# Output projection by seven block products, its sums prepared in the attention stage, two blocks of results added by DMAs

## The chip, the cores and the metric

One core of one Trainium2 chip runs the whole program. The metric is the device time of one execution in microseconds. The core has a matrix engine (PE, with its weight loads as PEld), a vector engine (DVE), a scalar engine (ACT), a general engine (POOL), and an engine that issues DMAs (SP). Each takes its own instructions in order and waits for the others by semaphores. PE writes to eight banks of PSUM, each 128 x 512 fp32.

## The reference

One decoder layer on 1024 positions with width 1024, all fp32:

```python
h = rms_norm(x, ln_pre_mix[l])
proj = h @ w_in[l]                       # pooling channels (256), then q, k, v of 12 heads of 64
...
pool_out = multi_scale_pool(u_pool, w_pool[l], pool_scale[l])
attn_out = dilated_attention(q, k, v).reshape(B, S, ATTN_WIDTH)
mix = jnp.concatenate([pool_out, attn_out], axis=-1) @ w_out[l]
x = x + rms_norm(mix, ln_post_mix[l])
h = rms_norm(x, ln_pre_ffn[l])
f = (jax.nn.silu(h @ w_gate[l]) * (h @ w_up[l])) @ w_down[l]
x = x + rms_norm(f, ln_post_ffn[l])
```

The change concerns the line with `w_out`: a 1024 x 1024 matrix times the 1024 mixed channels of 1024 positions.

## The kernel before

Everything lies channels by positions: a tile has 128 channels (a chunk) on its partitions and 512 positions (half h = 0 or 1) in its rows. Each fp32 factor is split into a high part (what the matrix engine's reduced fp32 keeps) and a low part (the rest), and a product is three matrix instructions: high by high, high by low, low by high (`PASSES`). ACT makes high parts, DVE or POOL low parts, by a subtraction (`split`, line 335; on POOL it is cut into two instructions of 512 columns).

The program runs in four stages.

1. **Projections and attention**, 0 to about 410 us. There are twelve units (pair of heads, half); each makes scores, exponents, turned exponents and products with v. A plan gives each unit's steps times in units (`put`, line 1184; the numbers are in the table `PRM`), and `emit` (line 1135) sorts all steps by these times. That sort is the order of each engine's instructions. Dense work that needs no fresh attention result (projections of the next pair, and at the end the output projection) is dealt between the steps as fill (`Fill`, line 595).
2. **Output projection** (`out_proj`, line 1271): for each half h and each 128 output channels d, eight input chunks k by three passes, so 24 instructions of 128 x 512 that collect in one bank, 192 for a half. Half 0 is fill in the last units, with its chunk 7 (from the last pair) last. Half 1 comes after the attention, from 414 to 460 us. Each result bank is copied by ACT to `z[h](d)` in SBUF (line 1298). The input chunks are written by `into` as high and low parts, sent to memory by `to_memory` (`mixd`) and fetched by `mixed` when their room comes free; only chunk 7 stays in SBUF.
3. **Norm and residual** (`chain`, line 1397): `Squares` sums the squares of a half's eight rows (ACT squares, DVE adds), PE's product with a column of ones gives the mean, ACT, POOL and PE turn it into a row of factors (`rsqrt_mean`, line 358: the power -1/2 is one POOL instruction), `add(d)` scales z and adds x on DVE (lines 1410, 1411), `parts(d)` makes the parts of the scaled sum for the next stage, and `whole(d)` its squares and scaled copy. For half 0 this runs beside the second half of the output projection; for half 1 it runs beside the first feature products. In half 1, ACT squares the projection's results straight from the banks.
4. **Features (SwiGLU)**: 2816 features in pairs j of blocks, by seven block products of quarter size in place of eight (`seven`, line 1588). For the first six pairs, the product that needs only half 0 of the positions is made first (`firsts`, line 1484; 48 instructions a pair, first with the four upper input chunks, block row kh = 0, then with the lower). The list that is handed to `emit` at line 1708 sets their order.

SP's order is set by the same sort, so a DMA that waits for its source holds back those behind it.

## Time and profile before

| what | us |
|---|---|
| median of three runs (lowest, highest) | 1110.75 (1110.72, 1111.95) |
| the profiled execution | 1109.44 |
| its span on the core (rest lies around it: 1.84) | 1107.6 |
| PE busy in the span | 1093.1 |
| DVE, ACT, POOL busy | 784.7, 550.3, 528.8 |
| stretch 100 to 400 us (attention): PE, DVE, ACT, POOL busy of 300 | 295.5, 242.4, 212.5, 128.0 |
| stretch 400 to 460 us (end of attention, second half of the projection): the same, of 60 | 60.0, 44.3, 39.9, 7.6 |
| stretch 460 to 530 us (first feature products): the same, of 70 | 70.0, 63.9, 43.4, 5.0 |

A row of the timeline reads: start and duration in us, engine, line, operation, output from input by the program's names, size, and the count of instructions in the row. Its duration runs to the modelled end of the last; the pace of a row of PE is found from the start of the next row. In a table of windows, "(x304)" is the number of instructions, and PEclk the granted clock of PE as a share of full speed.

### The profile page before, as it was taken

The page shows a single profiled execution, that of the slowest core. Times are in us where ns is not written, and L with a number is a line of the kernel's source. Part 1 is how long each engine was busy: PE and PEld are TensorE (multiplying, and loading weights), DVE is VectorE, ACT ScalarE, POOL GpSimd, SP SyncE. Part 2 cuts the span into 40 slices and gives each one's busy share as a digit, 9 for nine tenths or more (in the row PEclk, how much of TensorE's full clock was granted, in tenths as well). Part 3 has the DMA queues.
Part 4 walks back from the last instruction along what each step waited for, and adds up shares of the span by engine and source line. Part 5 has one row for each costly group of instructions (what it writes and reads, how often), then busy time and mean ns, then how long its engine had stood idle before and what let it go on. Part 6 is the DMA issues. An engine that isn't in the chain of part 4 may idle for free.

```text
span 1107.6 us, 16113 instructions
## 1 busy us (share of the span) xinstructions
PE 1093.1 (99%) x5694; PEld 932.1 (84%) x5694; DVE 784.7 (71%) x1356; ACT 550.3 (50%) x985; POOL 528.8 (48%) x425
## 2 busy tenths in 40 slices
PE   9999999999999999999999999999999999999997
PEld 7888899989888888888888888888888888888896
DVE  7967978787988767799777777677566462343684
ACT  7456767676777755866322222333222543343442
POOL 0111617263554021100567777576568986666521
PEclk9999999999999999999999999999999999999999
DMA  8325242425149437664466666543445895656442
GB/s 295 96 75 189 96 134 75 155 70 178 55 156 336 154 142 288 240 228 156 160 235 238 238 238 237 199 171 124 152 185 210 285 353 194 208 180 201 133 153 77
DMA packets 91297, 201.82 MB, mean 182 GB/s; under 512 B 9296, under 2 KB 25168, under 8 KB 89808
## 3 DMA queue, kind: packets, MB, share of 16 engines
q1 hardware_dynamic: 90240, 200.00, 51.4%
q8 instruction: 45, 0.74, 0.3%
q10 hardware_dynamic: 976, 0.79, 0.2%
q14 instruction: 36, 0.29, 0.1%
HBM read 143.87 MB, written 56.89 MB: 181 GB/s over the span
## 4 chain that ended last, share of the span: by engine, by line
PE 89%; DVE 5%; ACT 2%; POOL 2%; DMA 1%; issue 1%; ACTq 0%; DVEq 0%; POOLq 0%
PE ps_pj L292 26%; PE ps_s L292 25%; PE ps_o L292 25%; PE ps_t L292 10%; PE ps_t L295 2%; POOL whl L340 1%; DMA v<-vd 1%; DVE pp L912 1%; DVE ptr L966 0%; DVE ql L561 0%; ACT ptr L965 0%; DMA wraw<-in_w_in_dram 0%; DVE rsw L529 0%; DVE qh L560 0%; ACT pp L830 0%
## 5 line engine op out<-in xcount | busy, mean ns | idle before, releaser
L292 PE MATMUL ps_o<-tT,fw 128*128 128x512 f32 x648 | 150.4, 389 | 0.0
L292 PEld LDWEIGHTS ps_o<-tT,fw 128*128 128x128 f32 x648 | 121.6, 188 | 25.2
L292 PE MATMUL ps_pj<-x,whl 128*128 128x512 f32 x480 | 131.4, 399 | 0.2 <-DVE whl L340 0.2
L1482 POOL TENSOR_TENSOR fw<-rw,fw 128x512 fp32r<-128x512 f32 x72 | 99.0, 1397 | 30.4 <-ACT fw L1480 28.9
L292 PEld LDWEIGHTS ps_pj<-x,whl 128*128 128x128 f32 x480 | 86.4, 188 | 14.6 <-DVE whl L340 0.7
L340 POOL TENSOR_TENSOR whl<-wraw,whl 128x512 fp32r<-128x512 f32 x44 | 60.2, 1389 | 67.0 <-ACT whl L336 62.3
L1777 POOL TENSOR_TENSOR op<-rw,op 128x512 fp32r<-128x512 f32 x38 | 62.2, 1637 | 32.7 <-ACT op L1776 32.3
L366 POOL TENSOR_TENSOR nrr<-nrr,half 128x4 f32<-128x4 f32 (+1 forms) x7 | 6.9, 985 | 141.8 <-ACT eps L365 99.2
L292 PE MATMUL ps_s<-b,fw 128*128 128x512 f32 x312 | 72.5, 389 | 0.0
L1482 POOL TENSOR_TENSOR whl<-rw,whl 128x512 fp32r<-128x512 f32 x30 | 47.8, 1613 | 45.5 <-ACT whl L1480 30.8
L292 PEld LDWEIGHTS ps_s<-b,fw 128*128 128x128 f32 x312 | 58.6, 188 | 12.1
L1776 ACT ACTIVATE op<-rw 128x1024 fp32r<-128x1024 f32 x38 | 40.0, 1058 | 57.3 <-PE ps_t L292 29.8
L1480 ACT ACTIVATE fw<-rw 128x1024 fp32r<-128x1024 f32 x45 | 47.5, 1061 | 38.6 <-PE ps_o L292 15.5
L292 PE MATMUL ps_pj<-whl,x 128*128 128x256 f32 (+1 forms) x432 | 64.7, 298 | 0.0
L966 DVE TENSOR_TENSOR ptr<-ps_t,ptr 128x512 fp32r<-128x512 f32 (+1 forms) x84 | 52.9, 647 | 15.1 <-ACT ptr L965 14.7
L965 ACT ACTIVATE ptr<-ps_t 128x512 fp32r<-128x512 f32 (+1 forms) x84 | 45.2, 561 | 32.9 <-PE ps_t L295 23.5
L292 PEld LDWEIGHTS ps_pj<-whl,x 128*128 128x128 f32 x432 | 57.3, 191 | 2.2
L1778 DVE TENSOR_TENSOR op<-rw,op 128x512 fp32r<-128x512 f32 x33 | 28.9, 875 | 40.7 <-ACT op L1776 36.6
L1777 POOL TENSOR_TENSOR fw<-rw,fw 128x512 fp32r<-128x512 f32 x26 | 42.6, 1640 | 21.1 <-ACT fw L1776 20.5
L830 ACT ACTIVATE pp<-pp,sx 128x256 f32<-128x256 f32 x96 | 47.8, 501 | 8.2 <-DVE sx L827 7.7
L292 PE MATMUL ps_o<-ptr,v 128*128 128x128 f32 (+3 forms) x376 | 50.5, 268 | 1.2 <-DVE ptr L966 0.8
L292 PE MATMUL ps_pj<-b,fw 128*128 128x512 f32 x216 | 50.3, 389 | 0.0
(337 smaller groups left out, 2780.9 us busy)
## 6 DMA issues: line engine op xcount, KB each, us to landing
rw<-bd SPq DMA_DIRECT2D x77, 256.0 KB, 3.9
rw<-in_w_gate_dram SPq DMA_DIRECT2D x28, 512.0 KB, 4.7
rw<-in_w_up_dram SPq DMA_DIRECT2D x28, 512.0 KB, 6.0
v<-vd SPq DMA_DIRECT2D x22, 512.0 KB, 4.9
rw<-wsd SPq DMA_DIRECT2D x44, 256.0 KB, 3.8
bd<-p SPq DMA_DIRECT2D x39, 256.0 KB, 2.4
rw<-in_w_down_dram SPq DMA_DIRECT2D x33, 256.0 KB, 3.8
wraw<-in_w_out_dram SPq DMA_DIRECT2D x15, 512.0 KB, 5.3
```

Of the source, the lines that this page charges most:

```text
L292: return tc.keep_in_program_order(nc.tensor.matmul(*a, **k))
L295: return tc.keep_in_program_order(nc.tensor.transpose(dst, src, by))
L340: pin(eng.tensor_tensor(dst[:, 1, at:at + w], src[:, at:at + w], dst[:, 0, at:at + w].bitcast(F32), ALU.subtract))
L830: nc.scalar.activation(pt[:, j, lo:], pt[:, j, lo:], AF.Exp, bias=sx[:, 0, side, j, hd, 0:1], scale=-1.0, accum_out=sx[:, 0, side, j, hd, ...
L912: nc.vector.tensor_scalar(pv, pv, un.wv[:, side, j, hd:hd + 1], None, op0=ALU.mult)
L965: nc.scalar.activation(ptr[:, 0, :w], t[:, :w], AF.Copy)
L966: nc.vector.tensor_tensor(ptr[:, 1, :w], t[:, :w], ptr[:, 0, :w].bitcast(F32), ALU.subtract)
L1480: nc.scalar.activation(dst[:, :, 0], src, AF.Copy)
L1482: low[0] = eng.tensor_tensor(dst[:, i, 1], src[:, i], dst[:, i, 0].bitcast(F32), ALU.subtract)
L1776: nc.scalar.activation(w[:, :, 0], raw, AF.Copy)
L1777: nc.gpsimd.tensor_tensor(w[:, 0, 1], raw[:, 0], w[:, 0, 0].bitcast(F32), ALU.subtract)
L1778: (nc.gpsimd if p == "P1" else nc.vector).tensor_tensor(w[:, 1, 1], raw[:, 1], w[:, 1, 0].bitcast(F32), ALU.subtract)
```

## The change

The 1024 x 1024 product is written as 2 x 2 blocks of 512 (output channels, input channels, positions) and made by seven products of such blocks in place of eight. Four are of weight and input sums (S1 by T1, S2 by T2, S3 by T3, S4 by B22), three of blocks themselves (A11 by B11, A12 by B21, A22 by T4). Each is 4 output tiles i by 4 chunks c by 3 passes, so 48 instructions and 336 in all, where there were 384.

- **Order of products.** P5, P3, P1, P6, P7 (240 instructions, list `early`) are the fill of the last units; P2, P4 (96, `later_on`) come after the attention, where half 1 stood. Half 1 of the positions is block column 1, half 0 is block column 2. Half 0 is complete after the early products, half 1 only with P2 and P4.
- **Input sums.** `finish` runs when a chunk of 128 channels is done (pooling chunks 0 and 1, pairs 2 to 7). It makes that chunk's blocks and sums, their parts, and sends them to memory (`mixd`, now seven blocks by four chunks). Values of other chunks that a sum needs come back from memory by `other_chunks` (`vald`, `t2d`). The table 'se' says which engine, DVE (1) or POOL (0), makes each. Two tiles, `job` and `val`, exist once each.
- **Weight sums.** `weight_sums` reads w_out, makes the four sums S1 to S4 on POOL, four times four instructions of 128 x 512, in the same tile `job`, and sends them to memory (`wod`) during the attention. `out_weights` fetches weights for two output tiles at a time and splits them by 'oe' on DVE or POOL.
- **Results.** `out_done`: a product that comes first for a z row is copied there by ACT; later ones are added by DVE. P2 and P4 are copied by ACT to the tile `late`, and four DMAs on POOL's queue add it to half 1's z in SBUF (`accum_op`), two rows each. The squares of half 1 are taken from z after that, through one tile, `rb`.
- **Moved.** `whole`, the mean and its row of half 0 go from beside the projection to beside the first feature products. These are ordered in groups: for pairs 0 to 2 the products with kh = 0, then those with kh = 1, then pairs 3 to 5 as before. Table `PRM`: several hundred planned times and engine choices are new.

```diff
- 'c0': (0.14731, 0.21299, 0.22594, 0.57089, 0.30506, 0.69439, 0.95539, 0.04332),
- 'ft': ('pj', 't', 's', 'pj', 't', 's'),
+ 'c0': (0.24652, 0.35, 0.44694, 0.95, 0.1, 0.1745, 0.26633, 0.28),
+ 'ft': ('t', 's', 'pj', 't', 's', 'pj'),
...
+ 'se': {'B11': (1, 0, 0), 'B22': (1, 0, 0, 0, 0), 'B21': (1, 1, 0)},
...
+ 'oe': (0, 1, 0, 0, 1, 0, 0, 0, 0, 0, 1, 0, 0, 1),
+ 'zp': 200}
...
+    def finish(k, h, val):
+
+        c, v = k % 4, val.bitcast(F32)
+        if k < 4:
+            nc.sync.dma_start(vald[h, c], v)
+            did(("val", h, c))
+            if h == 0:
+                return
+        t = job["t"]
+        x = [t[:, i].bitcast(F32) for i in range(2)]
+        name = "B11" if k < 4 else "B21" if h else "B22"
+        eng = [nc.vector if i else nc.gpsimd for i in G["se"][name]]
+        hl = att.tile([P, 2, 512], F32R, name="mix", tag="mix", bufs=1)
+        halved(hl[:, 0], hl[:, 1], v, eng[0])
+        ship(name, c, hl.rearrange("p a t -> p (a t)"))
+        if name == "B22":
+            eng[1].tensor_tensor(x[0], v, x[0], ALU.subtract)
+            eng[2].tensor_tensor(x[1], x[0], x[1], ALU.add)
+            nc.sync.dma_start(t2d[c], x[1])
+            did(("t2", c))
+            halved(t[:, 2], t[:, 0], x[0], eng[3])
+            ship("T3", c, t[:, 2], t[:, 0])
+            halved(t[:, 3], val, x[1], eng[4])
+            ship("T2", c, t[:, 3], val)
+            return
+        i = k if k < 2 else 0
+        eng[1].tensor_tensor(x[i], *((x[i], v) if name == "B11" else (v, x[i])), ALU.subtract)
+        halved(t[:, 2 + i], t[:, i], x[i], eng[2])
+        ship("T1" if name == "B11" else "T4", c, t[:, 2 + i], t[:, i])
...
+    def weight_sums(i):
...
+            nc.gpsimd.tensor_tensor(to, a, b, op)
+        nc.sync.dma_start(wod[i].rearrange("p n m -> p (n m)"), r.rearrange("p f m -> p (f m)"))
...
+    early = [(p, i) for p, j in (("P5", 2), ("P5", 0), ("P3", 0), ("P3", 2)) for i in (j, j + 1)]
+    early += [(p, i) for j in (0, 2) for p in ("P1", "P6", "P7") for i in (j, j + 1)]
...
+    later_on = [(p, i) for p in ("P2", "P4") for i in range(4)]
...
+    def out_done(p, i, ps, done):
+
+        def plus(h, d):
+            with tc.high_priority(offset=G["zp"]):
+                nc.vector.tensor_tensor(z[h](d), ps, z[h](d), ALU.add)
...
+        if p in ("P2", "P4"):
+            d = i + 4 * (p == "P4")
+            if i == 0:
+                late["y"] = fw([P, 4, 512], F32, "late")
+            nc.scalar.activation(late["y"][:, i], ps, AF.Copy)
+            if i % 2:
+                with tc.high_priority(offset=G["zp"]):
+                    nc.gpsimd.dma_start(z[1](d - 1, 2), late["y"][:, i - 1:i + 1], accum_op=ALU.add)
+                for e in (d - 1, d):
+                    done(e, z[1](e))
...
+                if (p, i) == ("P1", 0):
+                    for x in range(2):
+                        fetch_block("T2", x, xroom(6, 7))
...
-    sqs = [(Squares(), Squares(tag=("o", "pj")[h], to=eps[:, 4 * h:4 * h + 4])) for h in range(2)]
+    sqs = [(Squares(jk=(("p", 2), ("rb", 1))[h]), Squares(tag=("o", "pj")[h], to=eps[:, 4 * h:4 * h + 4])) for h in range(2)]
...
-    st, weights = out_proj(1, 3, sqs[1][0].add)
-    weights(3)
-    *chain0, mean0, rows0 = chain(0, *sqs[0], G["c0"])
-    emit((st, 0.0, 1.0), *chain0, mean0)
+    for n in range(2):
+        fetch_block("T4", n, lambda n: big(4 + n, [P, 2, 2, 512], F32R, "t4"))
+    st = out_proj(later_on, sqs[1][0].add)
+    *chain0, whole0, mean0, rows0 = chain(0, *sqs[0], G["c0"])
+    emit((st, 0.0, 1.0), *chain0)
...
-    emit(([x for f in before for x in f], 0.0, 1.0), (two[0], 1.0, 1.0 + part), (two[1], 1.0 + part, 1.0 + 2 * part),
-         *chain(1, *sqs[1], G["c1"]), rows0,
+    emit(([x for n in (0, 8) for f in before[:3] for x in f[n:n + 8]] + [x for f in before[3:] for x in f], 0.0, 1.0), (two[0], 1.0, 1.0 + part), (two[1], 1.0 + part, 1.0 + 2 * part),
+         *chain(1, *sqs[1], G["c1"]), whole0, mean0, rows0,
```

In instructions of the whole program: PE has 48 fewer matrix instructions of 512 columns; DVE goes from 1334 to 1313, ACT from 848 to 855, POOL from 430 to 503 (four of them the DMAs), SP from 522 to 592.

**First place: the fetch of T2 near the end of the attention.** SP in the kernel after; `fw` four times are B11 and T3, `m_4574` and `m_4576` the two halves of T2, `m_4054` the end of B22:

```order
L986 DMA t2d<-job 128x512
L965 DMA mixd<-job 128x512 x3
L965 DMA mixd<-val 128x512
L1346 DMA m_4054<-mixd 128x1024
L1368 DMA wraw<-wod 128x2x512
L955 DMA job<-t2d 128x512
L1346 DMA fw<-mixd 128x2x1024 x4
L1368 DMA wraw<-in_w_out_dram 128x2x512
L1346 DMA m_4574<-mixd 128x2x1024
L1346 DMA m_4576<-mixd 128x2x1024
```

Before, SP fetched the mixed chunks of half 1 there, with no writes of sums between them:

```order
L332 DMA wraw<-in_w_out_dram 128x1024 x3
L1262 DMA fw<-mixd 128x2x1024 x3
L332 DMA wraw<-in_w_out_dram 128x1024 x2
L931 DMA mixd<-mix 128x1024
L1262 DMA fw<-mixd 128x1024
```

T2's two halves now stand behind five other transfers in that queue.

**Second place: the two means of the projection.** PE in the kernel after, from the end of the early products on. The first row is the last 24 instructions of P7 and the first 24 of P2; the rows with `fw,ow` are the rest of P2, `t_4960` and `t_4962` are the block T4 of P4. Behind the rows shown stand the other 36 of P4, then 72 feature instructions, and then the mean of half 1:

```order
L305 MATMUL ps_pj<-fw,whl 128x512 x48
L305 MATMUL ps_o<-ones,sq 128x1 x4
L305 MATMUL ps_pj<-fw,ow 128x512 x10
L308 MATMUL ps_o<-idt,nrr 128x128 x4
L305 MATMUL ps_pj<-fw,ow 128x512 x14
L305 MATMUL ps_pj<-t_4960,whl 128x512 x6
L305 MATMUL ps_pj<-t_4962,whl 128x512 x6
```

and ACT there, the last squares of half 1 (`rb`), with those of half 0 (`p<-z`), scaled copies (L1533) and feature weights (L1585) between them:

```order
L1482 ACTIVATE rb<-z_4601 128x512
L1482 ACTIVATE p<-z_4131 128x512
L1585 ACTIVATE fw<-rw 128x2x512
L1533 ACTIVATE z_4131<-z_4131,g3s 128x512 x2
L1482 ACTIVATE rb<-z_4601 128x512
L1585 ACTIVATE fw<-rw 128x2x512
L1482 ACTIVATE rb<-z_4601 128x512 x2
L1604 ACTIVATE q<-ps_s 128x512 x2
L377 ACTIVATE nrr<-ps_o 128x4
```

Before, the last two squares of half 1 came straight from the banks, one of them behind half 0's mean:

```order
L1376 ACTIVATE p<-ps_pj 128x512
L361 ACTIVATE nrr<-ps_o 128x4
L365 ACTIVATE eps<-ps_o 128x4
L1298 ACTIVATE z_4851<-ps_s 128x512
L1376 ACTIVATE p<-ps_s 128x512
```

The work on half 0's rows, of which most stood beside the projection, now stands ahead of half 1's last squares on ACT.

**Third place: POOL from the last weights of the projection to the powers.** After:

```order
L356 TENSOR_TENSOR ow<-wraw,ow 128x512 x2
L356 TENSOR_TENSOR whl<-wraw,whl 128x512 x2
L1402 DMA z_4600<-late 128x1024
L382 TENSOR_TENSOR nrr<-nrr,half 128x4
L1402 DMA z_4600<-late 128x1024
L1402 DMA z_4601<-late 128x1024
L1587 TENSOR_TENSOR whl<-rw,whl 128x512 x2
L1587 TENSOR_TENSOR fw<-rw,fw 128x512 x2
L1402 DMA z_4601<-late 128x1024
L382 TENSOR_TENSOR nrr<-nrr,half 128x4 x2
```

Before, the three powers stood together there, behind the last splits of projection weights:

```order
L340 TENSOR_TENSOR whl<-wraw,whl 128x512 x2
L914 TENSOR_SCALAR pp<-pp,wv 128x256 x15
L340 TENSOR_TENSOR whl<-wraw,whl 128x512 x4
L366 TENSOR_TENSOR nrr<-nrr,half 128x4 x3
L1482 TENSOR_TENSOR fw<-rw,fw 128x512 x2
```

The first power now stands behind a DMA that adds to z, the next two behind four of them.

316 lines of the change are left out of this document (175 added, 141 removed), and 272 rows, old and new, of the table PRM.

## The prediction

> **What bounds the kernel now.** First the page's busy times and chain:
>
> ```profile
> PE 1093.1 (99%) x5694; PEld 932.1 (84%) x5694; DVE 784.7 (71%) x1356; ACT 550.3 (50%) x985; POOL 528.8 (48%) x425
> PE 89%; DVE 5%; ACT 2%; POOL 2%; DMA 1%; issue 1%; ACTq 0%; DVEq 0%; POOLq 0%
> ```
>
> PE bounds the whole, so a PE instruction taken away is worth its pace wherever PE then finds its factors. The windows say where that is:
>
> ```profile
> 100.00:400.00 300.00, 295.47 (x1908) 264.73 (x1908) 242.40 (x632) 212.46 (x509) 128.01 (x141) 1.00 0.40 140
> 385.00:390.00 5.00, 5.00 (x28) 4.13 (x27) 4.86 (x14) 2.53 (x7) 2.01 (x5) 1.00 1.03 421
> 400.00:460.00 60.00, 60.00 (x304) 50.72 (x303) 44.34 (x61) 39.90 (x65) 7.55 (x5) 1.00 0.63 233
> 460.00:530.00 70.00, 70.00 (x318) 57.93 (x318) 63.87 (x100) 43.44 (x71) 4.96 (x4) 1.00 0.54 194
> ```
>
> Columns are busy us (and count) of PE, PEld, DVE, ACT, POOL, then granted clock, DMA share, GB/s. From 400 to 530 PE never waits and POOL is nearly idle; DVE has 91% from 460 on. The clock is full, so no term of clock enters.
>
> The pace of a dense instruction of 512 columns, from the starts of two rows of the timeline:
>
> ```profile
> 483.98 11.04 PE L292 MATMUL ps_s<-b,fw 128*128 128x512 f32 x48
> 494.86 1.52 PE L292 MATMUL ps_pj<-b,fw 128*128 128x512 f32 x6
> ```
>
> (494.86 - 483.98) / 48 = 0.2267 us.
>
> **The change part by part.**
>
> *Fewer products.* 384 become 336. 48 x 0.2267 = **-10.9**. All stand in dense fill or in the dense stretch behind the attention.
>
> *The fetch of T2.* SP issues it behind B11 and T3 (4 MB) and 0.5 MB of weights. Those wait for room that the last scores leave. In before the same room is released so, and the end of the attention has these rows:
>
> ```profile
> 378.74 0.28 PE L292 MATMUL ps_s<-k,ql 128*128 128x256 f32 x1
> ...
> 390.96 1.03 PE L295 MATMUL ps_t<-idt,pp 128*128 128x128 f32 x8
> 391.75 3.01 PE L292 MATMUL ps_s<-m,whl 128*128 128x512 f32 x12
> 394.60 0.87 PE L292 MATMUL ps_o<-ptr,v 128*128 128x128 f32 x8
> 395.30 0.85 PE L292 MATMUL ps_o<-ptr,vlast 128*128 128x128 f32 x8
> ...
> 379.98 1.40 SPq L1262 DMA_DIRECT2D fw<-mixd  x3
> ...
> DMA to landing us min/median/max: 4.8/6.9/8.8
> ```
>
> The first megabyte lands 4.8 us after its issue, and at 421 GB/s each further one takes 2.5 (1.049 MB / 421); the extremes 4.8 and 8.8 of the three, issued 0.9 apart, bear that out. So T2's first half, with 4.5 MB ahead of it, lands 4.8 + 3 x 2.5 + 1.2 + 2.5 = 16.0 after the issue, and the issue follows the last scores (end 379.0) by about 1.0: **17.0**. PE wants it behind 48 instructions of 512 columns (10.9), 26 of attention products (0.70 per eight, the starts of 394.60 and 395.30: 2.3) and 16 turns (0.79 per eight: 1.6), with 0.2 for two small ones: **15.0**. That is +2.0; bounds 0 (PE is late itself) and 4 (the writes of sums take bandwidth too).
>
> *The end of the early products to the first rows.* Call the end of P7 E. In before the chain of half 0's norm is, from mean to first sum:
>
> ```profile
> 421.00 0.95 PE L292 MATMUL ps_o<-ones,sq 128*128 128x1 f32 x8
> 424.68 0.60 PE L295 MATMUL ps_o<-idt,nrr 128*128 128x128 f32 x4
> 425.31 5.36 DVE L1410 SCALAR_TENSOR_TENSOR z<-z,g2s,ps_o 128x512 f32<-128x512 f32 x8 [3.84 <-PE ps_o L295]
> 430.59 4.89 DVE L1411 TENSOR_TENSOR z<-z,xr 128x512 f32<-128x512 f32 x8
> 435.40 1.21 DVE L340 TENSOR_TENSOR whl<-wraw,whl 128x1024 fp32r<-128x1024 f32 x1
> 436.54 0.74 DVE L1421 SCALAR_TENSOR_TENSOR b<-z,g3s,b 128x512 fp32r<-128x512 f32 x1
> 440.21 4.05 DVE L1421 SCALAR_TENSOR_TENSOR b<-z,g3s,b 128x512 fp32r<-128x512 f32 x6
> ```
>
> PE does 24 of P2 first (mean at E+5.4), then 10 more beside the mean's way through ACT and POOL (0.8 + 2.3: row at E+8.5), and DVE starts 0.6 behind, at E+9.2. It does eight scalings at 0.66 (5.28 to the next start), eight sums at 0.60 (4.81) and the split of the weights for P4's tiles 2 and 3 (1.14): done at E+20.4. PE wants that low part behind 72 instructions and the small ones, at E+17.9: a stall of **2.5**; in before, such splits stood one in front of the other with banks to spare.
>
> *The mean of half 1.* In before it came without a wait:
>
> ```profile
> 457.56 0.95 PE L292 MATMUL ps_o<-ones,sq 128*128 128x1 f32 x8
> ```
>
> After, PE reaches it behind 96 instructions of P2 and P4, 72 of features and the small ones: 168 x 0.2267 = 38.1, plus 1.1, so E+39.2 without stalls. It needs eight squares of half 1, and ACT makes the last of them behind all that stands ahead in its order. ACT's prices, as intervals between starts:
>
> ```profile
> 436.10 0.63 ACT L1376 ACTIVATE p<-z 128x512 f32<-128x512 f32 x1
> 436.62 0.60 ACT L1376 ACTIVATE p<-ps_s 128x512 f32<-128x512 f32 x1
> 437.10 0.61 ACT L1298 ACTIVATE z<-ps_pj 128x512 f32<-128x512 f32 x1
> 437.57 3.80 ACT L1420 ACTIVATE b<-z,g3s 128x512 fp32r<-128x512 f32 x6
> 441.25 0.60 ACT L1298 ACTIVATE z<-ps_s 128x512 f32<-128x512 f32 x1
> ```
>
> A square is 0.52, a copy from a bank 0.48, a scaled part (3.68 / 6) 0.61; scaled copies to z are taken as the same. A split of weights is 0.95:
>
> ```profile
> 456.54 1.05 ACT L1480 ACTIVATE whl<-rw 128x1024 fp32r<-128x1024 f32 x1
> 457.49 0.58 ACT L1376 ACTIVATE p<-ps_s 128x512 f32<-128x512 f32 x1
> ```
>
> The first part can start with the first finished sum, at E+9.2 + 5.3 + 0.6 = E+15.1. From there to the last square ACT has 8 parts (4.9), 16 squares of both halves (8.3), 8 scaled copies (4.9), 8 weight splits (7.6), three copies to `late` and two results (2.4): 28.1 us, so E+43.2, and the last addition and its release bring E+44.1. That is **4.9** behind E+39.2, with the 2.5 above inside it. If ACT and DVE hand the one `rb` tile to and fro with a wait each time (an addition of 0.6 behind each of the later squares, about half seen by ACT), it is 2 more, 6.9; if ACT finds its work in less than these sums, nothing: bounds 0 and 7.8. DVE alone has 31.8 us by the same rows from E+9.2 (E+41), so ACT ends last. I take the sum that needs no hand-over, 4.9.
>
> *Additions by DMA.* Four on POOL's queue, 512 KB each. No row shows such a DMA. Nearest: a power on POOL, and writes of that size and less.
>
> ```profile
> 422.24 1.02 POOL L366 TENSOR_TENSOR nrr<-nrr,half 128x4 f32<-128x4 f32 x1 [2.45 <-ACT nrr L361]
> ...
> mixd<-mix SPq DMA_DIRECT2D x14, 512.0 KB, 4.4
> bd<-p SPq DMA_DIRECT2D x39, 256.0 KB, 2.4
> ```
>
> Landing within 4.4 us, the first lies ready at E+16 or so and the last before ACT comes to its squares (E+41), so 0. If POOL is held by an issue ahead of a power, up to 2 (a power is 1.0 us long here); below zero no reason. I take 0, as the power waits for PE's mean behind 24 products anyway. The Trainium skill, "DMA: Bandwidth & Descriptors", section on the anatomy of a DMA from GpSimd, gives 2.0 us plus bytes by 436 GB/s; by it an estimate is 3.2 us each, and the sum would be the same.
>
> *The attention.* DVE loses 20 low parts of `mix` and some splits and gains sums, about 10 us less. ACT has 6 more. POOL gains 44 instructions of sums and parts, 8 weighings and 10 splits:
>
> ```profile
> L340 POOL TENSOR_TENSOR whl<-wraw,whl 128x512 fp32r<-128x512 f32 x38 | 51.1, 1366 | 34.4 <-ACT whl L336 29.8 <-issue 4.6
> L914 POOL TENSOR_SCALAR pp<-pp,wv 128x256 f32<-128x256 f32 x46 | 24.6, 553 | 50.1 <-DVE wv L883 50.1
> ```
>
> 54 x 1.37 + 8 x 0.55 = 78 us more on POOL, so 128 + 78 = 206 of 300. PE there runs under its dense pace already, and its idle of 4.5 us in the window is the least that lighter DVE could give back: between -3 and +6, from what hides it (POOL has 94 us left) to what shows (next part). Taken as 0.
>
> *At no cost:* new banks for the first features and groups of three pairs (the same 288 instructions), and `whole` of half 0 later (its 8 additions lie in DVE's 31.8).
>
> Sum: -10.9 + 2.0 + 4.9 = **-4.0**. The profiled 1109.44 becomes 1105.4; the median of the runs lies 1.3 above the profiled one, so **1106.7**.
>
> **The rivals.**
>
> *Nearly the whole saving arrives.* The means and T2 are hidden after all: ACT's squares come early since PE itself ran late. For it: PE at 60.00 and 70.00 of 60 and 70, so before had slack in every hand-over there. Against: DVE's 63.87 of 70. Time: 1110.75 - 10.9 = 1099.9, to 1102 with half of one stall.
>
> *The saving is eaten.* Hand-over by one `rb` tile (6.9), T2 at its 4: -10.9 + 10.9 = 0, 1110.8.
>
> *POOL gates the attention (slower).* In before, a DVE addition took twice as long while POOL split:
>
> ```profile
> 416.25 3.54 POOL L340 TENSOR_TENSOR whl<-wraw,whl 128x512 fp32r<-128x512 f32 x2 [3.51 <-ACT whl L336]
> 418.56 1.78 DVE L1377 TENSOR_TENSOR sq<-sq,p 128x512 f32<-128x512 f32 x1
> 439.00 1.28 DVE L1377 TENSOR_TENSOR sq<-sq,p 128x512 f32<-128x512 f32 x2
> ```
>
> 1.78 against 0.61 to 0.64. The added 62 instructions of two inputs or weighings, each making one DVE instruction about 0.7 to 1.1 longer, are 43 to 68 us of DVE time against 57.6 idle (300 - 242.4) and 10 saved. It decides if more than 6 of them fall on work for which PE waits; at 11 (a sixth to a quarter) the time is 1106.7 + 11 = 1117. SP adds to this: it waits for POOL's sums in order, with v's and T3's transfers behind them. Against it: POOL is more than half idle in that window. The Trainium skill, "SBUF — State Buffer", section "Who interferes with whom", says the same more strictly: a DVE instruction with two SBUF inputs and a GpSimd one that reads SBUF exclude one another for the whole instruction. The two rows agree with it; it speaks against this change, and by it alone this rival would be the likelier.
>
> *The change does not do what it says* has no room: the count of 48 instructions is in the order.
>
> **How the numbers follow.** Forecast (1104 to 1108.5) 0.43; nearly whole (1098.5 to 1104) 0.19; eaten (1108.5 to 1113) 0.15; slower (above 1113, to 1117 and more) 0.23. About 0.2%, 2.2 us, is what a measurement can tell from no change. Range: 1098.5, the whole saving with 1.4 of the attention's possible gain, to 1114.5, which leaves out the larger part of the slower case, 0.17, and 0.03 below. Faster 0.61 (0.19 + 0.42), same 0.16, slower 0.23. The likeliest one's own range is 1104 to 1108.5.
>
> **What would show it.** In the profile after: PE waits in the 45 us behind P7 of 4 to 7 us, one for DVE's split ahead of P4's tile 2, and one ahead of half 1's mean, released by DVE's last `sq<-sq,rb`; a wait of about 2 for a DMA at the first instruction on T2; PE as dense as before from the row of half 1 on; POOL at about 206 of 300 in the attention. It is wrong if PE's idle time in the attention grows by more than 4 us, if an accumulating DMA takes over 10 us so that the squares wait for it, or if no wait shows behind P7.

## The result: slower by 2.7%, in four stretches

The kernel after takes 1141.92 us (1137.31 to 1142.47), the kernel before 1110.74 beside it: a ratio of 1.0274 (1.0261 to 1.0287); every ratio below is to the kernel before, run beside the kernel in question. The profiled execution took 1141.82, with a span of 1140.0 us. The prediction, 1106.7 with a range to 1114.5, was wrong in size and in sign.

The page of the kernel after, busy times:

```profile
PE 1099.6 (96%) x5646; PEld 933.2 (82%) x5646; DVE 803.3 (70%) x1335; ACT 557.3 (49%) x992; POOL 634.9 (56%) x498
```

PE has 48 instructions fewer and yet 6.5 us more busy time, and it idles 40.4 us where it idled 14.5. The same events cut the span of both kernels into four: the end of the last scores, the mean of half 0, the mean of half 1 behind its residual, the end. (Where a time of "the last scores" is given below, it is the start of the last row `ps_s<-k,ql`: 378.74 before, 396.03 after.) First before, then after; columns as in the windows of the prediction (stretch, its length, then busy us and count of PE, PEld, DVE, ACT, POOL, clock, DMA share, GB/s):

```profile
0.00:379.02 379.02, 371.54 (x2281) 327.72 (x2282) 302.73 (x743) 258.35 (x597) 136.92 (x151) 1.00 0.42 144
379.02:421.00 41.98, 41.98 (x253) 36.23 (x253) 28.43 (x51) 25.70 (x46) 9.94 (x11) 1.00 0.55 204
421.00:532.30 111.30, 111.30 (x511) 92.41 (x509) 98.09 (x151) 72.60 (x117) 5.99 (x5) 1.00 0.61 221
532.30:1107.60 575.30, 568.28 (x2654) 475.76 (x2652) 355.44 (x415) 193.65 (x226) 375.90 (x258) 1.00 0.57 198
```

```profile
0.00:396.31 396.31, 374.68 (x2263) 329.00 (x2264) 319.99 (x733) 262.89 (x602) 199.85 (x196) 0.99 0.55 193
396.31:455.91 59.60, 57.37 (x316) 48.80 (x315) 34.48 (x54) 30.14 (x52) 25.80 (x23) 0.97 0.79 292
455.91:558.20 102.29, 95.13 (x408) 77.93 (x406) 93.48 (x129) 69.14 (x112) 26.46 (x19) 0.93 0.69 239
558.20:1140.00 581.80, 572.39 (x2666) 477.49 (x2664) 355.30 (x420) 195.09 (x228) 382.79 (x260) 1.00 0.57 198
```

The difference in PE's count, times 0.2267 us, says how much longer or shorter each stretch should be; the rest is lost:

| stretch | longer by | PE instructions more | should be | lost |
|---|---|---|---|---|
| attention, to the last scores | +17.3 | -18 | -4.1 | 21.4 |
| to half 0's mean | +17.6 | +63 | +14.3 | 3.3 |
| behind the early products | -9.0 | -103 | -23.3 | 14.3 |
| the rest | +6.5 | +12 | +2.7 | 3.8 |

Together 42.8 us are lost and 10.4 gained by the counts. (In the attention the 18 missing instructions are all of 512 columns, so the price fits.) Two things stand out. In the attention, DVE has 17 us more work, not 10 less, and POOL 63 more. And the clock is no longer full: 0.99, 0.97 and 0.93. The mean granted clock of the whole is 0.987, where before had 0.999: some 14 us of 1140. The trace's record of the clock shows where. Between 5 us and the tail of the program it is at one half in five spells, which start at 117.4, 141.3, 407.5, 472.4 and 499.7 us and last 6.83, 3.41, 3.41, 3.41 and 10.24 us: 27.3 in all, of which half is lost. In the kernel before there is no such spell.

Of PE's waits after, the view of waits names these (in all, times, longest):

```profile
PE ps_o L305 <- DVE sq L1483: 5.1, 1, 5.1
PE ps_o L305 <- DVE ptr L1042: 4.5, 5, 1.6
PE ps_pj L305 <- DVE whl L356: 3.4, 3, 1.8
PE ps_t L308 <- POOL pp L930: 2.7, 1, 2.7
PE ps_pj L305 <- DVE z L1377: 2.2, 1, 2.2
PE ps_pj L305 <- DMA m<-mixd: 2.2, 1, 2.2
```

The first and the wait of 1.8 in the third row are the two that were forecast behind the early products. The others lie in the attention and its end. The wait of 2.2 us for DVE's `z` and the spell of half clock behind it (1.7) more than make up the 3.3 us lost on the way to half 0's mean; what costs the last stretch 3.8 us was not followed.

### The profile page after: what moved, and what is told of

It is laid out like the page before. It is cut to its first block, busy times and chain, and to the rows that moved or that the text cites. A ratio compares the mean times of both kernels' runs of the same rounds, so it can differ in the third digit from the quotient of the medians.

```text
span 1140.0 us, 16282 instructions
## 1 busy us (share of the span) xinstructions
PE 1099.6 (96%) x5646; PEld 933.2 (82%) x5646; DVE 803.3 (70%) x1335; ACT 557.3 (49%) x992; POOL 634.9 (56%) x498
## 4 chain that ended last, share of the span: by engine, by line
PE 45%; POOL 2%; DVE 1%; issue 1%; DMA 1%; SPq 0%; DVEq 0%; ACT 0%; POOLq 0%
PE ps_o L305 18%; PE ps_s L305 13%; PE ps_pj L305 9%; PE ps_t L305 5%; POOL fw L1587 1%; DMA rw<-in_w_up_dram 1%; POOL whl L1686 1%; POOL whl L1587 1%; DVE tT L1660 0%; DMA rw<-in_w_gate_dram 0%; DVE sq L1483 0%; DVE wraw L1699 0%; DVE p L1608 0%; DVE rw L1701 0%; DVE y L1992 0%
## 5 line engine op out<-in xcount | busy, mean ns | idle before, releaser
L1587 POOL TENSOR_TENSOR fw<-rw,fw 128x512 fp32r<-128x512 f32 x76 | 107.8, 1442 | 31.7 <-ACT fw L1585 30.5
L1587 POOL TENSOR_TENSOR whl<-rw,whl 128x512 fp32r<-128x512 f32 x36 | 58.7, 1650 | 63.6 <-ACT whl L1585 58.3
L356 POOL TENSOR_TENSOR whl<-wraw,whl 128x512 fp32r<-128x512 f32 x46 | 64.2, 1418 | 22.2 <-ACT whl L352 22.1
L1585 ACT ACTIVATE fw<-rw 128x1024 fp32r<-128x1024 f32 x45 | 47.4, 1059 | 38.4 <-PE ps_o L305 15.4
L305 PE MATMUL ps_pj<-b,fw 128*128 128x512 f32 x264 | 61.5, 389 | 0.0
L305 PE MATMUL ps_s<-b,fw 128*128 128x512 f32 x264 | 61.5, 389 | 0.0
L305 PEld LDWEIGHTS ps_s<-b,fw 128*128 128x128 f32 x264 | 49.5, 188 | 10.3
L305 PEld LDWEIGHTS ps_pj<-b,fw 128*128 128x128 f32 x264 | 49.5, 188 | 10.3
L1882 POOL TENSOR_TENSOR fw<-rw,fw 128x512 fp32r<-128x512 f32 x26 | 42.6, 1640 | 21.4 <-ACT fw L1881 20.8
```

The costliest lines, as they stand in the source:

```text
L305: return tc.keep_in_program_order(nc.tensor.matmul(*a, **k))
L356: pin(eng.tensor_tensor(dst[:, 1, at:at + w], src[:, at:at + w], dst[:, 0, at:at + w].bitcast(F32), ALU.subtract))
L1585: nc.scalar.activation(dst[:, :, 0], src, AF.Copy)
L1587: low[0] = eng.tensor_tensor(dst[:, i, 1], src[:, i], dst[:, i, 0].bitcast(F32), ALU.subtract)
L1882: nc.gpsimd.tensor_tensor(w[:, 0, 1], raw[:, 0], w[:, 0, 0].bitcast(F32), ALU.subtract)
```

## The experiments

**What a wait of PE costs.** Both the late mean (5.1 us) and others are followed by rows with half the clock. In the kernel after, around the weighing that came 2.7 us late and around the mean:

```profile
112.00:118.00 6.00, 3.26 (x17) 2.42 (x16) 2.79 (x6) 2.11 (x5) 4.54 (x5) 0.95 0.27 109
118.00:124.00 6.00, 5.70 (x17) 4.33 (x18) 5.87 (x12) 2.58 (x4) 6.00 (x11) 0.50 0.11 42
...
494.00:500.00 6.00, 0.86 (x6) 0.47 (x4) 5.30 (x8) 3.92 (x7) 0.00 (x0) 0.97 0.62 218
500.00:510.00 10.00, 10.00 (x36) 8.73 (x37) 7.68 (x11) 3.17 (x7) 2.13 (x2) 0.50 0.43 163
510.00:516.00 6.00, 6.00 (x28) 4.95 (x27) 6.00 (x11) 2.85 (x4) 0.00 (x0) 1.00 0.36 116
```

So the wait was made by itself, in the kernel before, whose PE is dense there:

```diff
+HELD = 12
...
+    def held(sq):
+        for _ in range(HELD):
+            nc.gpsimd.tensor_scalar(sq.sq, sq.sq, 1.0, 1.0, op0=ALU.mult, op1=ALU.mult)
+        sq.mean()
...
-        return [([load], -1, 0), ([sq.mean], at[0], 0), ([sq.rows], at[1], 0),
+        return [([load], -1, 0), ([lambda: held(sq)] if h else [sq.mean], at[0], 0), ([sq.rows], at[1], 0),
```

> The kernel before with twelve multiplications by one of the sum of squares on the general engine ahead of half 1's mean, which is otherwise idle there. They end about 9.6 us behind the last square (462.9), at 472.6, where the mean stood at 467.6: a wait of about 5 us of the matrix engine in a dense stretch. Theory (a wait is followed by half clock): 1110.7 + 5 + 4 to 5 = 1119-1121. Rival (the wait alone counts): 1115-1116. Rival (time is made up later): 1111-1113.

Measured: 1119.77 (ratio 1.0086, 1.0069 to 1.0102), 9.4 us more than the 1110.38 beside it. The timeline and windows of that kernel:

```profile
473.55 1.87 PE L293 MATMUL ps_o<-ones,sq 128*128 128x1 f32 x8 [5.40 <-POOL sq L1400]
475.28 2.91 PE L293 MATMUL ps_pj<-b,whl 128*128 128x512 f32 x6
477.98 1.06 PE L296 MATMUL ps_o<-idt,nrr 128*128 128x128 f32 x4
478.69 3.38 PE L293 MATMUL ps_pj<-b,whl 128*128 128x512 f32 x12
```

```profile
470.00:475.00 5.00, 1.45 (x7) 1.46 (x8) 0.00 (x0) 0.00 (x0) 3.08 (x5) 0.76 0.90 355
475.00:480.00 5.00, 5.00 (x16) 4.13 (x17) 1.62 (x3) 2.09 (x3) 3.49 (x3) 0.55 0.01 3
```

A wait of 5.4 us, then six instructions in 2.7 us, twice their 1.36. The wait of 5.4 and 3.4 lost to a spell of 6.83 us at half clock are 8.8 of the 9.4 us, which is within the interval (7.7 to 11.3). The Trainium skill, "TensorE: Matmul & The Clock Gate", section "Part 1: The HAM clock gate", says that the clock is gated to half after an idle window of about 3.4 us and comes back after a busy one. The factor of one half and the return agree. The length does not quite: in the kernel after a wait of 2.74 us was enough (118 to 124 us above).

**The attention: weight sums.** They were left out (loads, sixteen POOL instructions, stores), with blocks of w_out in the place of the sums.

```diff
-    for i, at in enumerate(G["j2"]):
-        put([lambda i=i: weight_sums(i)], at, 0)
...
-            src = wod[2 * j:2 * j + 2, :, SUMMED_AT[a]].rearrange("i p m -> p i m")
+            src = w_out[2 * j:2 * j + 2, :, :4].rearrange("i p k m -> p i (k m)")
```

> The kernel after without its weight sums: the sixteen sums on the general engine, their loads and stores are left out, and the products take blocks of w_out in their place (so the product itself is not the reference's). Theory (queue): the sums stand ahead of the weighings in the general engine's order, and the matrix engine waits for those; then the waits of 2.7 and 1.6 us at 118 and 140 us and the half clock behind them go, and the time falls from 1141.9 to 1128-1134. Rival (port): only the general engine's total load counts, by what it takes from the vector engine; 16 of 62 added instructions of a loss of 21 us make 5 us, 1136-1138. Rival (neither): within 2 us of 1141.9.

Measured: 1136.79 (ratio 1.0236, 1.0221 to 1.0251), 5 us less. The last scores come 5.2 us earlier, at 390.8. This is the size of the second theory, though the place is that of the first: PE's wait for the late weighing (POOL's `pp<-pp,wv`) fell from 2.74 to 1.39 us and did not vanish. The run does not divide the two, nor the 8.4 MB of transfers that went with the sums (233.3 MB are moved in the kernel after, 224.9 here). POOL's order in the kernel after shows the queue: two instructions of the weight sums stand ahead of the weighings, and the first of them had waited 2.97 us for a transfer to memory.

```profile
113.46 1.28 POOL L1006 TENSOR_TENSOR job<-job 128x512 f32<-128x512 f32 x1 [2.97 <-DMA mixd<-mix]
114.70 1.26 POOL L550 TENSOR_TENSOR rco<-rco,rsw 128x512 f32<-128x512 f32 x1
115.92 1.26 POOL L1006 TENSOR_TENSOR job<-job 128x512 f32<-128x512 f32 x1
117.17 3.72 POOL L930 TENSOR_SCALAR pp<-pp,wv 128x256 f32<-128x256 f32 x6
```

How far can the last scores of one trace be trusted? Five edits further below change only what stands behind the attention: a later mean, two tiles, additions on DVE, fewer squares, and the last two together. Up to the last scores they have the same instructions as the kernel after, in the same order on PE and SP and with a few neighbours exchanged on the other engines. Their last scores come at 393.1, 391.3, 393.4, 396.6 and 395.1, against 396.0 in the kernel after. So between variants of that kernel a step of less than some 5 us in the last scores of single traces shows nothing by itself, and the medians of the whole carry the argument there. The kernel before is steadier: 378.7, and 379.0 and 379.1 in two kernels with the same attention.

**The attention: load on POOL alone.** The kernel before, with POOL work that nobody waits for. In the first attempt the order of the program put all 44 instructions ahead of 90 us, so it measured the head of the program and not the attention:

```diff
+    nc.gpsimd.memset(spare, 0.0)
+    put([lambda: nc.gpsimd.tensor_tensor(spare, spare, spare, ALU.subtract)] * 44, 1.0, 11.5)
```

> The kernel before with 44 more instructions of two SBUF inputs on the general engine (504 columns of a tile that nothing reads), spread over units 1 to 11.5. They are waited for by nothing but what stands behind them in that engine's order. Theory (port and queue of the general engine cost the attention its 21 us): 1125-1135. Rival (the sums' own place on the path costs it, not the engine's load): 1111-1115.

Measured: 1135.37 (ratio 1.0225, 1.0210 to 1.0240). All of it was lost before the first scores, which came at 81.0 us and not at 56.6. DVE's instructions there, before and then with the load (minimum, median, maximum in ns):

```profile
L427 DVE SCALAR_TENSOR_TENSOR x<-xraw,g1s,x x10: 747/1276/1285, 4.6 to 21.8; 128x1024 fp32r<-128x1024 f32 x6, 128x512 fp32r<-128x512 f32 x4
```

```profile
L427 DVE SCALAR_TENSOR_TENSOR x<-xraw,g1s,x x10: 1382/2044/2046, 4.7 to 33.6; 128x1024 fp32r<-128x1024 f32 x6, 128x512 fp32r<-128x512 f32 x4
```

The second attempt tied the load to each unit's result:

```diff
                 if hd and pr.p < NPAIR - 1:
                     to_memory(un.mix, 2 + pr.p, h)
+                    nc.gpsimd.tensor_tensor(spare, un.mix[:, 0, :504].bitcast(F32), spare, ALU.subtract)
+                    for _ in range(3):
+                        nc.gpsimd.tensor_tensor(spare, spare, spare, ALU.subtract)
```

> The kernel before with four instructions of two SBUF inputs on the general engine behind each of ten attention units (40 in all, about 53 us of that engine), the first reading the unit's finished mix, so that they lie where the kernel after makes its input sums. Nothing waits for them but that engine's next work. Theory (the general engine's load costs the attention, by the port that the vector engine shares and by its queue): 40 of 62 instructions of a loss of 21 us, 1120-1130. Rival (the sums cost by standing in the chain from a unit's values to the next product): 1110-1114.

Measured: 1121.60 (ratio 1.0095, 1.0080 to 1.0110), 10.5 us more; the last scores come at 390.9, 12.2 later than before. So POOL work that no one waits for takes some 12 us of the attention, more than half of the 21.4. Up to the last scores DVE is busy 316.4 us where it was busy 302.7, with the same work. PE's waits that grew, before and then with the load:

```profile
PE ps_o L292 <- DVE ptr L966: 0.8, 2, 0.5
PE ps_o L292 <- DMA v<-vd: 0.2, 1, 0.2
```

```profile
PE ps_o L292 <- DVE ptr L967: 6.0, 7, 1.9
PE ps_o L292 <- DMA v<-vd: 2.4, 1, 2.4
```

So most of what PE waits longer is for DVE, but not all. One DVE group shows the way, here before, with the load, and in the kernel after:

```profile
L554 DVE TENSOR_TENSOR k<-rcl,k x20: 684/687/1012, 102.6 to 313.2; 64x512 fp32r<-64x512 f32 x20
```

```profile
L555 DVE TENSOR_TENSOR k<-rcl,k x20: 684/1021/1869, 102.9 to 319.3; 64x512 fp32r<-64x512 f32 x20
```

```profile
L570 DVE TENSOR_TENSOR k<-rcl,k x20: 684/847/1695, 103.4 to 326.4; 64x512 fp32r<-64x512 f32 x20
```

An instruction of 0.69 us takes up to 1.87. In the three traces every one of these that took longer than 0.69 us overlaps an instruction of POOL, and those that overlap none took 0.69. DVE's additions with one operand in a bank (`ptr<-ps_t,ptr`) kept their 0.68 us in all three kernels. This is what the Trainium skill, "SBUF — State Buffer", section "Who interferes with whom", states, and the rule by which alone, as the prediction said, the slower case would have been the likelier.

**The attention: the sums on DVE in place of POOL.** One line, 'se' all ones.

> The kernel after with all input sums and their low parts on the vector engine (28 instructions of 128 x 512 moved from the general engine, about 38 us of it, to about 20 us of the vector engine). Theory (the general engine's load and the shared port cost the attention): 1128-1137. Rival (the vector engine is what the attention waits for): 1145-1155.

Measured: 1159.43 (ratio 1.0427, 1.0411 to 1.0442), 17.5 more than the kernel after; last scores at 404.8. The rival holds: DVE is what the attention waits for. POOL's load hurts because it lengthens DVE's work; moving it onto DVE hurts more.

**The attention: the values' additions.** They read both halves by classes of positions, one from a bank and one from SBUF, and take 1.08 us. First all in plain order (which computes positions in another order), then only ACT's copy written by classes, which computes the same as the kernel after:

```diff
-                nc.scalar.activation(low, o[hd][64:128], AF.Copy)
+                nc.scalar.activation(low.rearrange("p (r c) -> p r c", c=4), by_class(o[hd][64:128]), AF.Copy)
...
-                                        by_class(low), ALU.add)
+                                        low.rearrange("p (r c) -> p r c", c=4), ALU.add)
```

> The kernel after, in which a unit's values are added into the tile in plain order and not by classes of positions (so positions of the attention's output are in another order, and the output is not the reference's). The 24 additions took 1.08 us, against 0.69 for those of the kernel before. Theory (vector engine's time in the attention is on the path): 24 x 0.39 = 9.4 us of it, of which half shows with its share of the clock, 1135-1138. Rival (it has idle time to hide that): 1140-1143.

> The kernel after, with one half of a unit's values written by classes where ACT copies it from the bank, so that the vector engine's addition reads SBUF in plain order; what is computed stays the same. Theory (the strided SBUF read makes the 24 additions 1.08 us long, and the vector engine's time is on the path): they fall to about 0.69 us, and the time to that of the plain order, 1133.6 (1132-1136). Rival (the strided write or the read of the bank is what is slow): 1139-1143, additions at 1.0 us and more.

Measured: 1133.61 (ratio 1.0204, 1.0188 to 1.0219) and 1136.57 (1.0223, 1.0190 to 1.0255). The additions, first in the kernel after, then with ACT's copy by classes:

```profile
L1086 DVE TENSOR_TENSOR val<-ps_o,low x24: 1037/1078/1117, 109.5 to 433.5; 64x512 f32<-64x512 f32 x24
```

```profile
L1086 DVE TENSOR_TENSOR val<-ps_o,low x24: 669/683/685, 109.8 to 429.1; 64x512 f32<-64x512 f32 x24
```

With the bank read in strides in both, it is the strided read of SBUF that makes the difference: ACT pays nothing for the strided read of the bank (0.596 us in both), and DVE's own strided read of the bank costs nothing either. 24 x 0.39 = 9.5 us of DVE; the whole is 5.4 us shorter with the second form and 8.3 with the first, and the last scores come 4.1 and 5.2 us earlier. The median of the second lay 0.6 above its expectation, with runs from 1132.4 to 1138.9.

**Do these add?** Weight sums left out and additions in plain order:

> The kernel after without the weight sums and with the values' additions from plain order; the product is not the reference's. If the two parts of the attention's loss are separate: 1110.9 + 31 - 5.3 - 5.1 = 1131 (1129-1133); if one covers the other, 1135-1137.

Measured: 1132.33 (ratio 1.0193, 1.0177 to 1.0210). By the times of the whole they are two parts: 9.6 us less than the kernel after, against 5.1 and 5.4 alone. The last scores come at 387.7, 8.3 us earlier, against 5.2 and 4.1.

**All sums and low parts left out**, with the high parts sent twice (and the weight sums' 8.4 MB of transfers gone, as above):

```diff
         nc.scalar.activation(hi, src, AF.Copy)
-        eng.tensor_tensor(lo, src, hi.bitcast(F32), ALU.subtract)
...
-            eng[1].tensor_tensor(x[0], v, x[0], ALU.subtract)
-            eng[2].tensor_tensor(x[1], x[0], x[1], ALU.add)
...
```

> The kernel after with none of the sums: neither weight sums nor input sums nor the low parts of the blocks are made (44 instructions of the general engine and 16 of the vector engine left out; high parts are sent twice in place of high and low, so the projection is not the reference's). Every high part on ACT, every transfer of blocks and all of PE's work stay. Theory (the sums' load on the general and vector engines is what the attention loses, with 9 us of the strided additions left): the last scores come at 382-386 us (396.0 after, 378.7 before), the whole at 1126-1131. Rival (the transfers, and SP's waits in order, cost the attention): last scores at 391 or later, 1136 or more.

Measured: 1138.48 (ratio 1.0256, 1.0237 to 1.0274). Half of it came as the theory had it: last scores at 385.0, 11 us earlier. The other half did not: the whole gains only 3.4 us. Its stretches say where the rest went:

```profile
0.00:385.30 385.30, 372.08 (x2263) 326.60 (x2264) 298.87 (x721) 261.16 (x601) 137.61 (x154) 1.00 0.52 180
385.30:444.10 58.80, 56.43 (x314) 47.53 (x313) 31.10 (x51) 29.04 (x53) 19.16 (x19) 1.00 0.77 295
444.10:554.30 110.20, 97.62 (x407) 79.00 (x406) 96.18 (x129) 68.83 (x110) 32.77 (x21) 0.91 0.63 209
```

The third stretch took 110.2 us, eight more than in the kernel after, for as many instructions of PE (407 and 408), with a clock of 0.91. In this kernel most of the gain ahead is given back there; with the weight sums alone left out, or the plain additions, the same stretch takes 101 to 103 us.

**The stretch behind the early products.** Five edits, each on another suspect. Mean of half 1 later and the last split on POOL (the numbers of 'c1' and 'c2' plus 0.09, the last of 'oe' 0):

> The kernel after with the norm of half 1 and the sums behind it 0.09 later in the planned order (26 more feature instructions ahead of its mean) and the split of the last weights on the general engine. Theory (a wait counts with the half clock behind it): the waits of 5.1 and 1.8 us and as much again for the clock go, 1128-1131. Rival (waits alone count): 1134-1136. Rival (the late squares only move the wait to the block sums of the next stage): 1140-1143.

Measured: 1145.01 (ratio 1.0316, 1.0300 to 1.0331). The wait at the mean is gone, and PE waits 5.9 us for the next stage's weights, split by ACT. This is nearest to the last rival: the wait moved, but to weights and not to block sums, and the time lies above its range.

Two tiles in place of the one `rb`:

> The kernel after with two tiles for the squares of half 1 in place of the one, rb. Theory (the sum of ACT's work makes half 1's mean late, not the hand-over): the wait of 5.1 us stays above 3.5, 1138-1142. Rival (hand-over by one tile): the wait falls by 2 and more, and with the half clock behind it 1134-1138.

Measured: 1144.86 (ratio 1.0306, 1.0288 to 1.0325). The wait at the mean fell from 5.1 to 3.1, as the rival said, but the time did not: a wait of 3.7 us for DVE appears at a bank of the first features. Neither theory had that.

The additions on DVE from the banks, in place of the DMAs:

```diff
-            nc.scalar.activation(late["y"][:, i], ps, AF.Copy)
-            if i % 2:
-                with tc.high_priority(offset=G["zp"]):
-                    nc.gpsimd.dma_start(z[1](d - 1, 2), late["y"][:, i - 1:i + 1], accum_op=ALU.add)
-                for e in (d - 1, d):
-                    done(e, z[1](e))
+            plus(1, d)
+            done(d, z[1](d))
```

> The kernel after without the additions by DMA: the results of P2 and P4 are added to z by the vector engine from the banks, as those of P6 and P7 are (eight instructions of 0.66 us more on it, eight copies of 0.48 us fewer on ACT). Theory (ACT's work and the landing of the DMAs, 9.1 us each, bring the squares late): half 1's mean waits 2 us or less and its half clock goes, 1130-1136. Rival (the vector engine is the limit in that stretch): the wait stays at 4 and more, 1139-1146.

Measured: 1141.52 (ratio 1.0275, 1.0258 to 1.0292), the same as the kernel after. The wait at the mean is gone, and in its place stand two waits for banks behind DVE (6.0 together), one of 1.8 and one of 2.3 for ACT. With the plain additions as well:

> Both of the former edits. If they work on separate stretches and each as its theory says, their gains add: 1141.9 - 8 - 8 = 1126 (1122-1130). If one covers the other, 1131-1136.

Measured: 1141.12 (ratio 1.0265, 1.0248 to 1.0281). They did not add, and neither number came: here the gain of the plain additions was lost. PE waits for banks behind DVE (7.1 us in this stretch), and in the attention 3.3 for a weighing and 2.5 for v's transfer; the last scores come at 394.1, no earlier than without the plain additions.

Less work: seven of half 0's squares left out, without and with that edit:

```diff
-            s3.add(d, z[h](d))
+            if h or d == 0:
+                s3.add(d, z[h](d))
+            else:
+                s3.c = d
```

> The kernel after with seven of the eight squares of half 0's second norm left out (seven instructions of 0.52 us less on ACT, seven of 0.61 us less on the vector engine, in the 45 us behind the early products; the factors of that norm are not the reference's). Theory (the two engines have more to do there than the 168 instructions of PE cover): the wait of 5.1 us ahead of half 1's mean falls by 4 us or more, its half clock goes too, and no wait as long takes its place, 1131-1135. Rival (the landing of the DMAs that add to z brings the squares late): the wait stays at 4 and more, 1139-1143.

> The kernel after with the additions on the vector engine in place of DMAs and without seven of half 0's squares (not the reference's). Theory (two chains end together ahead of half 1's mean, the engines' work and the landing of the DMAs, so that taking one away leaves the other): the mean waits 1 us or less, where each edit alone left a wait as long elsewhere or at 4.5; waits for banks behind the vector engine stay (5 to 8), and the time is 1131-1138. Rival (PE simply has too little to do there): the sum of waits between 440 and 520 us stays at 9 or more, 1139-1143.

Measured: 1142.90 (ratio 1.0286, 1.0250 to 1.0322) and 1143.64 (1.0295, 1.0276 to 1.0314). In the first, the mean still waits 4.5 us, and ACT's last squares now wait for the DMA that adds to z:

```profile
494.48 0.63 ACT L1482 ACTIVATE rb<-z 128x512 f32<-128x512 f32 x1 [2.37 <-DMA z<-late]
```

In the second PE waits for banks three times (2.2, 1.8 and 5.0 us: 9.0), the rival's number. Whatever was taken from this stretch, its length did not fall: 102.3 us after, 102.9 and 105.6 in these two, 105.3 with DVE's additions alone, 104.0 with two tiles. So no single one of the tested causes holds it. What fits these runs is that PE has 96 instructions of the projection there where it had 192, and that work on half 0's and half 1's rows, in order on ACT and DVE, fills what they covered; this is an inference, since no run gave PE more to do.

**Everything left out together** (sums, low parts, strided additions, seven squares):

> The kernel after without all three: no sums and low parts of blocks, additions from plain order, and seven of the eight squares left out (not the reference's). If the causes named account for the whole: the saving of 10.9 shows but for what is left of the waits for banks and weights in the attention's end, 1105-1113. If a part as large is still unknown: above 1118.

Measured: 1133.15 (ratio 1.0200, 1.0177 to 1.0223): above 1118, so a part as large as those named is still unknown. Last scores at 384.0. Of the attention's 21.4 us, 12.0 are so accounted for (7 to 13, by the scatter of the last scores), and 9.4 are not. The trace of this kernel divides the 9.4: up to the last scores PE idles 12.4 us where it idled 7.5 before (4.9 more), one spell of 3.41 us at half clock costs 1.7, and 2.8 lie in neither. The waits that grew are those for `ptr` (4.0 us in all, 0.8 before) and `dhl` (2.8, 0.8 before); PE waits for no transfer there. ACT does: 12.5 us for the values that `other_chunks` fetches and `finish` sends (`job<-vald` 8.3, `vald<-val` 3.2, `job<-t2d` 1.0), transfers that the kernel before does not have. Whether these waits are what PE pays for is not shown.

**Transfers.** The kernel before with 28 MB more of writes, four behind each mixed chunk:

```diff
         nc.sync.dma_start(mixd[h, k], x.bitcast(F32).rearrange("p a t -> p (a t)"))
+        for i in range(4):
+            nc.sync.dma_start(more[i], x.bitcast(F32).rearrange("p a t -> p (a t)"))
```

> The kernel before with four more writes of 512 KB to memory behind each of its fourteen mixed chunks (28 MB more, near the 31 MB that the kernel after moves more), issued by SP in its order. Rival (transfers and SP's order are the part of the attention's loss that stays, some 9 us, when sums, low parts and strided additions are gone): 1116-1122. Theory (they cost next to nothing, and the rest lies in the work of ACT and in the order of the units): 1110-1113.

Measured: 1128.85 (ratio 1.0151, 1.0129 to 1.0173), more than either expected; last scores at 399.0. The longest waits of PE in it are for v's transfer, queued behind a burst, and for turned exponents:

```profile
PE ps_o L292 <- DMA v<-vd: 5.6, 1, 5.6
PE ps_o L292 <- DVE ptr L969: 4.4, 2, 4.2
```

So 28 MB in SP's order can cost the attention 20 us when they come in bursts of 2 MB and hold the one `mix` tile. The kernel after spreads its 31 MB, and PE waited for no v there; its one wait for a transfer in the attention is that of 2.2 us, at 394.2, for the last chunk of B22. That transfers can cost the 9.4 us is shown; that they do in the kernel after is not.

**The groups of three pairs alone**, in the kernel before:

```diff
-    emit(([x for f in before for x in f], 0.0, 1.0),
+    emit(([x for n in (0, 8) for f in before[:3] for x in f[n:n + 8]] + [x for f in before[3:] for x in f], 0.0, 1.0),
```

> The kernel before with one part of the change alone: the first feature products in groups of three pairs, with the banks of the kernel after. Expected by all theories: no more than 2 us from 1110.7, since the instructions are the same; if the banks or the weights come late, waits in the stretch 460 to 530 us and up to 1120.

Measured: 1114.45 (ratio 1.0031, 1.0021 to 1.0041), 3.4 us slower, with a wait of 2.3 us for DVE at a bank of the first features. The prediction had put this at no cost.

No version was found that beats the kernel before. The one edit that keeps what is computed and makes the kernel after faster is ACT's copy by classes.

## Why the prediction was wrong, step by step

- **The saving (-10.9).** Right by the counts: 48 instructions fewer at the dense pace. What is lost elsewhere is four times that.
- **The attention ("Taken as 0", between -3 and +6).** This is the step that failed: 21.4 us. The prediction's own sign of being wrong came: PE's idle time up to the last scores grew from 7.5 to 21.6 us, by 14 and so by more than 4. DVE was to have 10 us less and had 17 more up to the last scores. Three terms were missed: 24 additions at 1.08 and not 0.69 (9.5 us of DVE; the whole 5.4 shorter without it), DVE instructions lengthened by POOL (`k`, 20 x 0.23, `qh`, 20 x 0.24, and others), and weighings queued behind weight sums (with the load of those sums 5.1 of the whole). The edits show 12.0 us of the 21.4, good to some 5 us; the rest stays open, with transfers as a candidate that was shown able to do it.
- **The rival "POOL gates the attention", 0.23.** It was the case that came, at about twice its price of 11. Its place and its mechanism are right in b_load2: DVE work lengthened by POOL, on which PE waits (6.0 us for `ptr`, where it waited 0.8). Its row was in the prediction (1.78 us against 0.64), and so was the page that stated the rule; both were weighed down by POOL's being "more than half idle". That is no argument, since what counts is whether DVE has time to spare at each of its steps. a_se, which relieved POOL and cost 17.5 us, shows that it has not.
- **The fetch of T2 (+2.0).** It did not wait: its room came free later than taken, and so did its use. A wait of 2.2 us came at the block ahead of it, B22's last chunk, which SP issues behind the writes of the sums. The size was right by chance.
- **The split of the last weights (2.5) and the mean of half 1 (4.9 with it).** The places were right and the waits came: 1.8 and 5.1. The sum was 7.2 with a wait of 0.2, near the upper bound. ACT's chain began at E+18.1 and not at E+15.1, since the weights to be split landed late (ACT waited 3.4 us for them), and the additions by DMA landed in 9.1 us and not in 4.4. The 0 for them hid that ACT's work and the landings end at nearly the same time, as a_lean shows. The hand-over of the one `rb`, which the sum left out at a price of 2 us, was real: with two tiles the wait at the mean fell from 5.1 to 3.1.
- **"No term of clock enters."** Wrong: each of these waits was paid about twice. Of 14.3 us lost in that stretch, 7.2 are PE's idle time and 6.8 the half of 3.41 and 10.24 us at half clock. The clock of before was full, and its PE hardly waits; one wait put into it (b_held12) brought half clock there too.
- **A row was read for another.** The mean at 457.56 us in before is half 0's second one; half 1's is the one at 467.56, five us behind its last square. It was used only to say that no wait stood there, and that holds for both.
- **Groups of three pairs at no cost.** 3.4 us by themselves, in the kernel before.

## What to carry to other kernels

Price a PE instruction taken away only after pricing what the engines beside it must do for it: with DVE at 80% of a stage, work on POOL with two SBUF operands is DVE work too (53 us of it made DVE busy 13.7 us longer here). Reckon with half clock behind a wait of PE of some 2 us or more: behind five waits in the kernel after it cost about as much again, behind two nothing. Compare the same point in several traces before a few microseconds at it are called an effect. When each cure of a wait only moves it, look at how much work PE has in that stretch in all.

## What the runs showed of the hardware that was not expected

- Half clock, exactly 0.50 in the windows, follows waits of PE of 1.60, 1.79, 2.23, 2.74 and 5.14 us, for 3.41, 3.41, 3.41, 6.83 and 10.24 us. These are one, two and three times 3.41 us, and the spells also start at multiples of 3.41 us from one another (141.27, 407.51, 472.36 and 499.67 lie 7, 85, 104 and 112 steps behind 117.37). Other waits as long (2.00 at 180.6 us, 2.21 at 394.2) left it at 1.00. What tells them apart was not tried.
- A DVE addition of 64 x 512 that reads its SBUF operand in strides of 512 bytes takes 1.08 us against 0.68, with its operand in a bank read in such strides both times; that stride in a bank costs nothing, for DVE or ACT.
- Four adding DMAs of 512 KB from POOL's queue landed 8.5 to 9.2 us after their issue, each issue holding POOL for 0.9 to 1.1 us, while plain transfers of that size around them took 9.0 to 10.5: with 340 GB/s moved in that stretch, the adding is not shown to cost anything of its own.
